# Second MLP products of the last half with tokens on partitions, in a two-layer encoder kernel

## The chip, the cores and the metric

The kernel runs on one core of one Trainium2 chip. Its time is device time in microseconds (us) of one execution; repeated executions of a kernel agree within some tenths of a per cent. Before the change the median of three runs is 1166.66 us (1165.98 to 1166.71).

## The reference

The input is one sequence of 512 tokens with 1024 channels, float32. Two layers follow each other; each has a mixer and an MLP, each wrapped in two RMS norms:

```python
x = x + rms_norm(m, g[1])                      # m: the layer's mixer on rms_norm(x, g[0])
h = rms_norm(x, g[2])
x = x + rms_norm(squared_relu_mlp(h, mlp_w1[i], mlp_w2[i]), g[3])

def squared_relu_mlp(h, w1, w2):               # 1024 -> 4096 -> 1024
    return jnp.square(jax.nn.relu(h @ w1)) @ w2

def conformer_conv(h, w_pw1, b_pw1, w_dw, b_dw, ln_g, ln_b, w_pw2, b_pw2):
    u = h @ w_pw1 + b_pw1                      # 1024 -> 2048
    a, g = jnp.split(u, 2, axis=-1)
    u = a * jax.nn.sigmoid(g)
    u = depthwise_conv(u, w_dw) + b_dw         # over tokens, centred, 31 wide
    u = jax.nn.silu(layer_norm(u, ln_g, ln_b))
    return u @ w_pw2 + b_pw2
```

Layer 0's mixer is a gated short convolution beside latent attention with 8 heads, with a shared input and a shared output projection. Layer 1's mixer is `conformer_conv`. The result is x after layer 1, float32.

## The kernel before

**Layout.** Channels lie on partitions and tokens along the free axis: x, the norm's output h, the MLP's hidden values and the sub-layer's output m are each 8 tiles of 128 channels by up to 512 tokens. A product therefore has a 128 x 128 block of a weight as the stationary operand and the tokens of one half as the moving one.

**Precision.** Every large product is made from three: a value is split into a part that the fast float32 mode of TensorE holds (`whi`, the high part of x) and a rest (`wlo`). `linear` (L252) and `mm` (L244) issue high x high, high x low and low x high, lines 248, 249 and 250, for each of eight blocks of input channels: 24 products make one output tile of 128 channels. This is called a step here.

**Weights.** `strip` (L212) loads 512 KB of weights on SP's queue (`raw`), copies the high part on ScalarE (L225) and subtracts the rest on GpSimd (L226). There are eight buffers for `whi` and eight for `wlo`. `take` (L552) asks for strips ahead of the step that uses them, as many as `AHEAD` says for the stage.

**Halves.** Work on the sequence is cut in two halves, A and B, so that one half's norms run beside the other half's products. Ahead of the depthwise convolution the halves are tokens 0 to 255 and 256 to 511. The convolution of A's last tokens would need 15 tokens of B, so behind it A2 is tokens 0 to 239 and B2 is 240 to 511 (`PAD` = 16, L118).

**Order.** The list M2 (L36) is the order of the middle part, and M3 (L37) of the last. An item is a run of steps (`up`: first MLP product of one of four groups of 1024 hidden channels, with relu, square and split; `down`: second product of that group, added to m; `pw1`, `pw2`: the convolution module's projections) or a chain of small work for one half (`join`: post-norm, add, next pre-norm; `norm`: the layer norm behind the convolution; `finish`: the last post-norm, add and store). While a chain is written out, `hold` and `pace` (L305 to L316) draw steps of the other half that come next in the list, so that TensorE has products beside it. The convolution is 31 multiply-adds per channel block on VectorE; `fill` (L278) credits each step with some microseconds (`FILL`) and puts in as many of the multiply-adds as the credit buys at the prices of `TAP_US`. What is left when `norm` begins is put in between further drawn steps, with `STEP_US - OP_US` = 1.96 us credited for each. The order on VectorE is the order written; on the other engines a planner may move an instruction ahead of one that it holds to be late.

**Accumulators.** Of the eight PSUM banks three are named S, two pj, one o and two mi. Products of `linear` go round S and pj, norms and transposes use o and mi.

**The end.** The last group of B2 ends with `down` (L535): add to m on VectorE, square on ScalarE, add to a sum, multiply by the post-norm's gain on ScalarE. `finish_step` (L952) then forms the column sums with products against ones (L370), the reciprocal root in small VectorE operations (`rstd`, L386 to L428), spreads it over partitions with products against the identity (L435), multiplies m by it and adds it to x, five of the eight tiles on VectorE and three on GpSimd, and stores each tile.

Of the kernel before, what the change touches and what calls it, by code (L numbers as in the profile page):

```python
# [35 lines left out]
M2 = [('up', 'A', 0, 0, 0, 8), ('join', 'B', 0, 1), ('down', 'A', 0, 0, 0, 8), ('up', 'A', 0, 1, 0, 8), ('down', 'A', 0, 1, 0, 8), ('up', 'A', 0, 2, 0, 8), ('down', 'A', 0, 2, 0, 8), ('up', 'A', 0, 3, 0, 8), ('down', 'A', 0, 3, 0, 8), ('join', 'A', 0, 3), ('up', 'B', 0, 0, 0, 8), ('down', 'B', 0, 0, 0, 4), ('pw1', 'A', 0, 8), ('down', 'B', 0, 0, 4, 8), ('up', 'B', 0, 1, 0, 8), ('down', 'B', 0, 1, 0, 8), ('up', 'B', 0, 2, 0, 2), ('norm', 'A'), ('up', 'B', 0, 2, 2, 8), ('down', 'B', 0, 2, 0, 8), ('pw2', 'A', 0, 8), ('join', 'A', 1, 1), ('up', 'B', 0, 3, 0, 8), ('down', 'B', 0, 3, 0, 8), ('join', 'B', 0, 3), ('up', 'A', 1, 0, 0, 8), ('down', 'A', 1, 0, 0, 4), ('pw1', 'B', 0, 8), ('down', 'A', 1, 0, 4, 8), ('up', 'A', 1, 1, 0, 8), ('down', 'A', 1, 1, 0, 8), ('up', 'A', 1, 2, 0, 6), ('norm', 'B'), ('up', 'A', 1, 2, 6, 8), ('down', 'A', 1, 2, 0, 8), ('up', 'A', 1, 3, 0, 4), ('pw2', 'B', 0, 8), ('join', 'B', 1, 1), ('up', 'A', 1, 3, 4, 8), ('down', 'A', 1, 3, 0, 8), ('up', 'B', 1, 0, 0, 8), ('down', 'B', 1, 0, 0, 6), ('finish', 'A'), ('down', 'B', 1, 0, 6, 8), ('up', 'B', 1, 1, 0, 8), ('down', 'B', 1, 1, 0, 8), ('up', 'B', 1, 2, 0, 8), ('down', 'B', 1, 2, 0, 8)]  # L36
M3 = [('up', 'B', 1, 3, 0, 8), ('down', 'B', 1, 3, 0, 8), ('finish', 'B')]  # L37
# [4 lines left out]
TAP_US = {T // 2 - PAD: (0.385, 0.51), T // 2 + PAD: (0.41, 0.54)}  # L42
# [9 lines left out]
IN_ORDER = ('M3',)  # L52
POOL_OUT = {'A': (), 'B': (0, 1, 2)}
AHEAD = {'m0': 7, 'm1': 2, 'm2': 4, 'm3': 5}
RAWS = {'m1': 4, 'm2': 4, 'm3': 1}
RAW0 = {'m1': 8, 'm2': 4, 'm3': 8}
# [34 lines left out]
class Seg:  # L91
# [28 lines left out]
STARTS = [0, 128, 256, 384, 112, 240, 368]  # L120
# [13 lines left out]
def trunk(ctx: ExitStack, tc: tile.TileContext, a, out: bass.AP):  # L134
# [32 lines left out]
    def accum():  # L167

        scope["turn"] += 1
        tags = [t for t in scope["acc"] if t != "pj" or not (convs or todo or scope.get("chain"))]  # L170
        return ps(tags[scope["turn"] % len(tags)])
# [4 lines left out]
    def scratch(w):  # L176
# [3 lines left out]
        tags = ["o", "pj", "mi", "pj"] if scope.get("chain") else ["o", "mi"]  # L180
# [5 lines left out]
    def ht(dt=F32):  # L186
        return new(ap, "h", 2 * NC, T + PAD, dt=dt)[:, :T]
# [4 lines left out]
    def hpair():  # L192
        return tuple(Win(new(ap, "h", 2 * NC, T + PAD, dt=F32R)) for _ in range(2))
# [6 lines left out]
    vec = cp.tile([P, NV], F32, name="vec")  # L200
    ident = kst[:, K_ID : K_ID + P]
# [70 lines left out]
    late, convs, todo, normed, credit, turn = [], [], [], [], [0.0], [0]  # L272
# [191 lines left out]
    def join(xs, ms, s, post, pre, hs, seg, h, mlp):  # L464
# [4 lines left out]
        hv = views(hs, seg)  # L469
# [51 lines left out]
    def up(w, hs, dst, seg):  # L521

        acc = linear(w, views(hs, seg), seg, whole=True)
# [631 lines left out]
```

## Time and profile before

| what | value |
|---|---|
| profiled execution, its own time | 1166.52 us |
| its span, first to last instruction | 1164.6 us |
| granted TensorE clock, mean | 0.996 |
| TensorE products (PE) | 1132.3 us busy, 8850 instructions |
| weight loads into TensorE (PEld) | 1093.1 us, 8850 |
| GpSimd (POOL) | 846.2 us, 409 |
| ScalarE (ACT) | 663.8 us, 1221 |
| VectorE (DVE) | 645.7 us, 1696 |
| read from HBM | 180.42 MB |

A line of the profile that names an operation reads: line of the kernel, engine, operation, tile written <- tiles read, then shapes and a count with x. Behind a bar stand the busy time in us, the mean duration of one in ns, and the time that the engine sat idle just ahead of these instructions, with what ended it. In a timeline the first two numbers are the start and the duration in us, and square brackets hold the idle time ahead and its releaser. In a table of windows the columns are the stretch, its length, the busy time of each engine asked for (with its instructions), the granted clock, the share of the DMA engines and GB/s. Products overlap each other: the duration of one is longer than the distance to the next.

### The profile page before, as it was taken

Reading aid. Unit: us, or ns where it says so; the run is one execution under the profiler, and the core shown is the slowest. Engines: PE = TensorE matmul, PEld = TensorE weight load, DVE = VectorE, ACT = ScalarE, POOL = GpSimd, SP = SyncE. Lnnn points to the kernel's source line nnn. Section 1 sums busy time; section 2 is a strip of 40 time slices with the busy share of each in tenths; the row PEclk is TensorE's granted clock in tenths of the full one; section 3 lists DMA queues with packets and bytes.
Section 4 is the critical chain, followed back from the end, with each engine's and each line's share of the span. In section 5 each row is a group of like instructions: output and inputs, shape, how many; then the busy total and the mean of one; then the engine's idle time right before and its main releaser. Section 6 shows DMA issues by size and latency. Waiting matters only on the chain.

```text
span 1164.6 us, 22863 instructions
## 1 busy us (share of the span) xinstructions
PE 1132.3 (97%) x8850; PEld 1093.1 (94%) x8850; DVE 645.7 (55%) x1696; ACT 663.8 (57%) x1221; POOL 846.2 (73%) x409
## 2 busy tenths in 40 slices
PE   7999989999999999999999999999999999999995
PEld 5788868999999999999999999999999999999995
DVE  5662699554522124499985265599985272322123
ACT  6531677466745457645566778546467685545352
POOL 5663563149988888598886978698887877887681
PEclk9999999999999999999999999999999999999998
DMA  6421332036656555366554555465655554653431
GB/s 209 156 85 30 101 106 73 1 116 231 205 179 198 182 180 187 126 219 195 178 188 161 182 181 191 151 212 192 198 182 181 173 174 161 213 179 123 150 131 39
DMA packets 55405, 183.99 MB, mean 158 GB/s; under 512 B 6401, under 2 KB 10881, under 8 KB 55297
## 3 DMA queue, kind: packets, MB, share of 16 engines
q1 hardware_dynamic: 54720, 181.86, 47.9%
q8 instruction: 69, 1.13, 0.4%
q10 hardware_dynamic: 576, 0.68, 0.2%
q14 instruction: 40, 0.32, 0.1%
HBM read 180.42 MB, written 2.10 MB: 157 GB/s over the span
## 4 chain that ended last, share of the span: by engine, by line
PE 92%; DVE 3%; ACT 3%; DMA 1%; issue 1%; POOL 0%; SPq 0%; POOLq 0%; ACTq 0%
PE S L248 23%; PE S L249 23%; PE S L250 22%; PE pj L248 7%; PE pj L249 7%; PE pj L250 7%; DVE pr L772 1%; PE mi L370 1%; PE mi L435 1%; ACT whi L225 1%; PE mi L775 1%; DVE s L766 1%; PE o L249 1%; PE o L250 0%; DVE pt L238 0%
## 5 line engine op out<-in xcount | busy, mean ns | idle before, releaser
L226 POOL TENSOR_TENSOR wlo<-raw,whi 128x1024 fp32r<-128x1024 f32 (+2 forms) x347 | 802.9, 2335 | 252.2 <-ACT whi L225 243.3
L225 ACT ACTIVATE whi<-raw 128x1024 fp32r<-128x1024 f32 (+2 forms) x347 | 355.7, 1031 | 378.0 <-PE S L249 176.6
L248 PE MATMUL S<-h,whi 128*128 128x256 f32 (+3 forms) x1216 | 346.8, 289 | 6.2 <-ACT h L232 3.4
L250 PE MATMUL S<-h,wlo 128*128 128x256 f32 (+3 forms) x1216 | 349.9, 289 | 0.0
L249 PE MATMUL S<-h,whi 128*128 128x256 f32 (+3 forms) x1216 | 349.8, 289 | 0.1
L248 PEld LDWEIGHTS S<-h,whi 128*128 128x128 f32 x1216 | 227.5, 189 | 12.2 <-ACT h L232 4.2
L249 PEld LDWEIGHTS S<-h,whi 128*128 128x128 f32 x1216 | 229.4, 189 | 4.3 <-DVE h L235 0.5
L250 PEld LDWEIGHTS S<-h,wlo 128*128 128x128 f32 x1216 | 229.5, 189 | 4.0 <-POOL wlo L226 0.3
L248 PE MATMUL S<-hid,whi 128*128 128x256 f32 (+2 forms) x824 | 230.3, 282 | 2.0 <-DVE acc L335 1.8
L249 PE MATMUL S<-hid,whi 128*128 128x256 f32 (+2 forms) x824 | 230.7, 281 | 0.0
L250 PE MATMUL S<-hid,wlo 128*128 128x256 f32 (+2 forms) x824 | 230.0, 280 | 0.0
L837 DVE SCALAR_TENSOR_TENSOR pj<-u,taps,pj 128x240 f32<-128x240 f32 (+1 forms) x464 | 192.4, 481 | 1.3
L248 PEld LDWEIGHTS S<-hid,whi 128*128 128x128 f32 x824 | 154.5, 189 | 2.8 <-DVE acc L335 2.2
L249 PEld LDWEIGHTS S<-hid,whi 128*128 128x128 f32 x824 | 155.4, 189 | 0.2 <-DVE hid L238 0.2
L250 PEld LDWEIGHTS S<-hid,wlo 128*128 128x128 f32 x824 | 155.4, 189 | 0.0
L248 PE MATMUL pj<-h,whi 128*128 128x272 f32 (+3 forms) x336 | 103.6, 308 | 6.9 <-ACT h L232 5.5
L249 PE MATMUL pj<-h,whi 128*128 128x272 f32 (+3 forms) x336 | 103.1, 307 | 0.0
L250 PE MATMUL pj<-h,wlo 128*128 128x272 f32 (+3 forms) x336 | 102.8, 306 | 0.0
L248 PEld LDWEIGHTS pj<-h,whi 128*128 128x128 f32 x336 | 63.7, 190 | 10.1 <-ACT h L232 5.8
L238 DVE TENSOR_TENSOR hid<-S,hid 128x256 fp32r<-128x256 f32 (+2 forms) x103 | 43.1, 419 | 51.2 <-ACT hid L232 50.9
L540 DVE TENSOR_TENSOR m<-S,m 128x256 f32<-128x256 f32 (+2 forms) x74 | 30.6, 416 | 65.3 <-PE S L250 65.3
L249 PEld LDWEIGHTS pj<-h,whi 128*128 128x128 f32 x336 | 63.6, 189 | 3.4 <-DVE h L235 0.9
(247 smaller groups left out, 1683.1 us busy)
## 6 DMA issues: line engine op xcount, KB each, us to landing
raw<-in_w SPq DMA_DIRECT2D x256, 512.0 KB, 3.4
raw<-in_pw SPq DMA_DIRECT2D x48, 512.0 KB, 3.4
raw<-in_win SPq DMA_DIRECT2D x16, 512.0 KB, 3.3
x<-in_xT SPq DMA_DIRECT2D x16, 256.0 KB, 4.2
raw<-in_wout SPq DMA_DIRECT2D x8, 512.0 KB, 3.3
raw<-in_wq SPq DMA_DIRECT2D x8, 192.0 KB, 2.4
out<-x SPq DMA_DIRECT2D x8, 120.0 KB, 2.6
out<-x SPq DMA_DIRECT2D x5, 136.0 KB, 1.7
```

What stands on the lines that cost most here:

```text
L225: nc.scalar.activation(h, r, AF.Copy)
L226: nc.gpsimd.tensor_tensor(out=lo[:, c0:c1], in0=r, in1=h.bitcast(F32), op=ALU.subtract)
L238: eng.tensor_tensor(out=lo, in0=src, in1=hi.bitcast(F32), op=ALU.subtract)
L248: nc.tensor.matmul(acc, sh, mh, start=i == 0, stop=False)
L249: nc.tensor.matmul(acc, sh, ml, start=False, stop=False)
L250: nc.tensor.matmul(acc, sl, mh, start=False, stop=i == n - 1)
L370: nc.tensor.matmul(s[:, b : b + 1], q[:, sl.start - self.seg.lo : sl.stop - self.seg.lo], one, start=i == 0, stop=i == len(self.parts) - 1,)
L435: nc.tensor.matmul(o[:, sl], r[:, b : b + 1].to_broadcast([bw, P]), ident[:bw, :bw], start=True, stop=True,)
L540: nc.vector.tensor_tensor(out=m[seg.sl], in0=acc, in1=m[seg.sl], op=ALU.add)
L766: nc.vector.reduce_max(out=mx, in_=S, axis=AX.X)
L772: eng.tensor_scalar(out=pr_, in0=pr_, scalar1=sm, scalar2=None, op0=ALU.mult)
L837: nc.vector.scalar_tensor_tensor(out=dst, in0=src, scalar=wk, in1=acc, op0=ALU.mult, op1=ALU.add)
```

## The change

**The last half's second products.** For B2 in layer 1 the `down` items become `turn` and `end`. The hidden tile's 128 x 128 block (128 hidden channels by 128 tokens) is now stationary, and 512 columns of a row strip of w2 are moving; the result has tokens on partitions and output channels along the free axis. Four banks are open through a group, one for each of two blocks of 128 tokens and two halves of the output channels (two S, two pj). A strip of w2 (128 hidden channels by 1024 outputs) serves 12 products. At a group's end the four banks are copied (ScalarE, first group) or added (VectorE) to tiles m of 128 x 512, which take the place of the convolution's u tiles.

**The residual.** A new item `residual` transposes x for B2 on TensorE, four times four blocks, and ScalarE copies the four banks into further u tiles.

**The end.** The last group goes by blocks of 128 tokens: all products of block 0 first, strip by strip, with all eight strips kept; then block 1, first its first 512 output channels, then its last 512 in two halves of 256. Each piece is added to m on VectorE, squared and summed along the free axis on ScalarE, and multiplied by the gain on GpSimd (a tile of the gain on all partitions is loaded once, on ScalarE's queue). The sum is then one number per partition, so the reciprocal root multiplies m directly in one operation that also adds the residual, and the rows are stored to a second output; the host puts the two outputs together.

**The halves.** Behind the convolution the halves are now 0 to 255 and 256 to 511, ahead of it 0 to 271 and 272 to 511. The shifted views of h are no longer needed. The stage M3 with its own buffers is gone: everything is in M2. `finish` now serves A alone and is done on VectorE.

```diff
-M2 = [...]
-M3 = [('up', 'B', 1, 3, 0, 8), ('down', 'B', 1, 3, 0, 8), ('finish', 'B')]
+M2 = [... ('up', 'B', 1, 0, 0, 8), ('turn', 'B', 1, 0, 0, 6), ('finish', 'A'), ('turn', 'B', 1, 0, 6, 8), ('up', 'B', 1, 1, 0, 8), ('residual', 'B'), ('turn', 'B', 1, 1, 0, 8), ('up', 'B', 1, 2, 0, 8), ('turn', 'B', 1, 2, 0, 8), ('up', 'B', 1, 3, 0, 8), ('end', 'B', 1, 3)]
...
-TAP_US = {T // 2 - PAD: (0.385, 0.51), T // 2 + PAD: (0.41, 0.54)}
+TAP_US = {T // 2: (0.395, 0.525)}
...
-AHEAD = {'m0': 7, 'm1': 2, 'm2': 4, 'm3': 5}
+AHEAD = {'m0': 7, 'm1': 2, 'm2': 4}
...
-HALVES = A, B = Seg(0, T // 2), Seg(T // 2, T)
-A2, B2 = Seg(0, T // 2 - PAD), Seg(T // 2 - PAD, T, PAD)
+HALVES = A, B = Seg(0, T // 2 + PAD), Seg(T // 2 + PAD, T)
+A2, B2 = Seg(0, T // 2), Seg(T // 2, T)
...
+    def banks_step(h, g):
+        if not turned:
+            for key in BLOCKS:
+                turned[key] = [None, tmp("u")[:, :T], tmp("u")[:, :T]]
+            turned["gain"] = gtok
+        for n, key in enumerate(BLOCKS):
+            turned[key][0] = ps(("S", "pj")[n % 2])
+    def turn_mm(acc, h, w, k, b, cols, n):
+        tok = slice(T // 2 + b * P, T // 2 + b * P + P)
+        x, c = hid[h][k], slice(cols.start + n, cols.stop + n)
+        return [
+            (acc[:, cols], x[0][tok], w[0][:, c], k == 0, False),
+            (acc[:, cols], x[0][tok], w[1][:, c], False, False),
+            (acc[:, cols], x[1][tok], w[0][:, c], False, k == NC - 1),
+        ]
+    def turn_step(tok, h, layer, g, k):
+        if k == 0:
+            banks_step(h, g)
+        w = take()
+        for b in range(2):
+            issue([turn_mm(turned[b, f][0], h, w, k, b, slice(0, T), f * T) for f in range(2)])
+        settle()
+        if k == NC - 1:
+            for key in BLOCKS:
+                acc, m, _ = turned[key]
+                if g == 0:
+                    nc.scalar.activation(m, acc, AF.Copy)
+                else:
+                    nc.vector.tensor_tensor(out=m, in0=acc, in1=m, op=ALU.add)
+    def residual_step(tok, h, b, f):
+        tp = misc()
+        lo = T // 2 + b * P
+        for i in range(NB):
+            nc.tensor.transpose(tp[:, i * P : (i + 1) * P], xs[f * NB + i].t[:, lo : lo + P], ident)
+        nc.scalar.activation(turned[b, f][2], tp, AF.Copy)
+    def end_step(tok, h, layer, g):
+        f12 = lack.pop(h)
+        banks_step(h, g)
+        ws = []
+        for k in range(NC):
+            ws.append(take())
+            issue([turn_mm(turned[0, f][0], h, ws[k], k, 0, slice(0, T), f * T) for f in range(2)])
+            settle()
+        parts = {b: [] for b in range(2)}
+        def piece(b, f, cols):
+            acc, m, _ = turned[b, f]
+            acc, m, g = acc[:, cols], m[:, cols], turned["gain"][:, f * T + cols.start : f * T + cols.stop]
+            nc.vector.tensor_tensor(out=m, in0=acc, in1=m, op=ALU.add)
+            sm = small(1)
+            nc.scalar.activation(acc, m, AF.Square, accum_out=sm)
+            nc.gpsimd.tensor_tensor(out=m, in0=m, in1=g, op=ALU.mult)
+            parts[b].append(sm)
+        def leave(b, r, n):
+            w = T // n
+            for f in range(2):
+                for i in range(n):
+                    m, x = (t[:, i * w : i * w + w] for t in turned[b, f][1:])
+                    nc.vector.scalar_tensor_tensor(
+                        out=x, in0=m, scalar=r, in1=x, op0=ALU.mult, op1=ALU.add
+                    )
+                    q = nc.scalar if i % 2 else nc.sync
+                    q.dma_start(out_b[b * P : (b + 1) * P, f * T + i * w : f * T + i * w + w], x)
+        def rest(f, cols):
+            for k in range(NC):
+                issue([turn_mm(turned[1, f][0], h, ws[k], k, 1, cols, f * T)])
+        for f in range(2):
+            piece(0, f, slice(0, T))
+        rest(0, slice(0, T))
+        r = root(0)
+        leave(0, r, 1)
+        piece(1, 0, slice(0, T))
+        for i in range(2):
+            cols = slice(i * T // 2, (i + 1) * T // 2)
+            rest(1, cols)
+            piece(1, 1, cols)
+        leave(1, root(1), 2)
...
+    nc.scalar.dma_start(gtok, a["gain"].to_broadcast([P, D]))
```

More of the change, by code (lines that the diff above doesn't have):

```diff
@@ L133, in trunk @@
 @with_exitstack
-def trunk(ctx: ExitStack, tc: tile.TileContext, a, out: bass.AP):
+def trunk(ctx: ExitStack, tc: tile.TileContext, a, out: bass.AP, out_b: bass.AP):
     nc = tc.nc
@@ L169, in accum @@
         scope["turn"] += 1
-        tags = [t for t in scope["acc"] if t != "pj" or not (convs or todo or scope.get("chain"))]
+        tags = [t for t in scope["acc"] if t != "pj" or turned or not (convs or todo or scope.get("chain"))]
         return ps(tags[scope["turn"] % len(tags)])
@@ L179, in scratch @@
         scope["scr"] += 1
-        tags = ["o", "pj", "mi", "pj"] if scope.get("chain") else ["o", "mi"]
+        tags = ["o", "pj", "mi", "pj"] if scope.get("chain") and not turned else ["o", "mi"]
         return ps(tags[scope["scr"] % len(tags)])[:, :w]
@@ L192, in hpair @@
     def hpair():
-        return tuple(Win(new(ap, "h", 2 * NC, T + PAD, dt=F32R)) for _ in range(2))
+        return tuple(Win(new(ap, "h", 2 * NC, dt=F32R)) for _ in range(2))
     def small(w=NB):
@@ L200, in trunk @@
     vec = cp.tile([P, NV], F32, name="vec")
+    gtok = cp.tile([P, D], F32, name="gtok")
     ident = kst[:, K_ID : K_ID + P]
@@ L521, in up @@
     def up(w, hs, dst, seg):
-        acc = linear(w, views(hs, seg), seg, whole=True)
+        acc = linear(w, hs, seg, whole=True)
         cols = slice(seg.lo, seg.lo + seg.n)
@@ L794, in trunk @@
         else:
-            attend(h, A if half == "A" else B)
+            attend(h, A2 if half == "A" else B2)
     ycat = ya + yb
@@ L930, in pw2_step @@
             sums[h] = Sum(NC, seg, whole=WHOLE[3])
-        acc = linear(take(), views(hs, seg), seg)
+        acc = linear(take(), hs, seg)
         nc.scalar.activation(ms[m][seg.sl], acc, AF.Identity, bias=col(V_BPW2 + m))
@@ L954, in finish_step, with add @@
         bc = rstds(sums[h], lack.pop(h))
[L955 to L971 removed]
+        def add(j, x, t):
+            nc.vector.tensor_tensor(out=x, in0=x, in1=t, op=ALU.add)
+            nc.sync.dma_start(out[j * P : (j + 1) * P, :], x)
+        for j in range(NC):
+            x, m = xs[j][seg.sl], ms[j][seg.sl]
+            t = scratch(seg.w)
+            nc.vector.tensor_tensor(out=t, in0=m, in1=bc, op=ALU.mult)
             settle()
@@ L975, in finish_step @@
         settle()
+    BLOCKS = [(b, f) for b in range(2) for f in range(2)]
+    def banks_step(h, g):
[13 more added lines that the diff above has]
+        ]
@@ new lines, in issue @@
+    def issue(lists):
+        for products in zip(*lists):
+            for acc, x, w, start, stop in products:
+                nc.tensor.matmul(acc, x, w, start=start, stop=stop)
+    def turn_step(tok, h, layer, g, k):
[12 more added lines that the diff above has]
+                    nc.vector.tensor_tensor(out=m, in0=acc, in1=m, op=ALU.add)
@@ L995, in run @@
                     add(down_step, h, *args, m)
+            elif what == "turn":
+                need(a["w2t"][args[1], k] for k in range(args[2], args[3]))
+                for k in range(args[2], args[3]):
+                    add(turn_step, h, *args[:2], k)
+            elif what == "residual":
+                for b, f in BLOCKS:
+                    add(residual_step, h, b, f)
+            elif what == "end":
+                need(a["w2t"][args[1], k] for k in range(NC))
+                add(end_step, h, *args)
             elif what == "wout":
@@ L1000, in run @@
                     add(shared_step, h, lambda: ycat, seg_of(h, 0), True, m)
-            elif what == "attend":
-                add(lambda tok, h, half: attend(h, A if half == "A" else B), *args)
             elif what == "pw1":
@@ L1044, in trunk @@
     run(M2)
-    ph.__exit__(None, None, None)
-    ph = phase("m3", raw=("raw2", RAWS["m3"], STRIP), **MLP)
-    run(M3, "M3" in IN_ORDER)
     ph.__exit__(None, None, None)
```

60 lines of the change are left out of this document (28 added, 32 removed).

## The prediction, made before the changed kernel ran

> **What bounds the kernel now.** First the page: busy times, then the chain that ended last.
>
> ```profile
> span 1164.6 us, 22863 instructions
> PE 1132.3 (97%) x8850; PEld 1093.1 (94%) x8850; DVE 645.7 (55%) x1696; ACT 663.8 (57%) x1221; POOL 846.2 (73%) x409
> ...
> PE 92%; DVE 3%; ACT 3%; DMA 1%; issue 1%; POOL 0%; SPq 0%; POOLq 0%; ACTq 0%
> ```
>
> PE is 92% of the chain: time is products times their pace, plus the places where PE stands, plus the tail behind the last product. The pace comes from three stretches with products of one width (busy time by windows: 256, 272 and 240 columns), and two rows of the first phase 18 products apart (512 columns).
>
> ```profile
> 340.00:400.00 60.00, 60.00 (x512) 1.00 0.60 194
> 960.00:1020.00 60.00, 60.00 (x483) 1.00 0.58 185
> 790.00:850.00 60.00, 60.00 (x535) 1.00 0.59 194
> ...
> 70.67 0.40 PE L248 MATMUL S<-h,whi 128*128 128x512 f32 x1
> ...
> 74.81 0.40 PE L248 MATMUL pj<-h,whi 128*128 128x512 f32 x1
> ```
>
> A count includes about two products under way at the window's start, so one product costs 60/510 = 0.1176 us at 256 columns, 60/481 = 0.1247 at 272, 60/533 = 0.1126 at 240; at 512 it is 4.14/18 = 0.230. A step (24 products) is 2.82, 2.99 and 2.70 us. A pair of unequal halves costs 5.69, an equal pair 5.64; 512 columns save 0.005 against two of 256.
>
> **The products.** Ahead of the convolution 88 step pairs (8 output projection, 64 MLP, 16 pw1) go from equal to unequal: 88 x 0.05 = +4.4 us. Behind it 40 pairs (8 pw2, 32 up) go the other way: -2.0. The 32 down steps of A grow from 240 to 256 columns: +3.8. The 32 down steps of B cost 32 x 2.99 = 95.7; they become 24 strips of 12 products at 512, 24 x 2.76 = 66.2, and the end: 72 at 512 and 48 at 256, 16.6 + 5.6 = 22.2. That is -7.3. Sum **-1.1**. No row has this pairing (a hidden tile stationary, weights moving), only the 512-wide rows above; at 0.226 it would be -2.5, at two 256-wide products' 0.235 it would be +0.7.
>
> In the old order a group's first down step reads all eight hidden tiles within 3 us, and PE waits for the last one:
>
> ```profile
> 1127.61 0.28 PE L250 MATMUL S<-hid,wlo 128*128 128x272 f32 x1
> 1127.89 1.05 ACT L225 ACTIVATE whi<-raw 128x1024 fp32r<-128x1024 f32 x1
> 1128.03 0.44 DVE L238 TENSOR_TENSOR hid<-S,hid 128x272 fp32r<-128x272 f32 x1 [0.46 <-ACT hid L232]
> 1128.05 0.52 PE L248 MATMUL S<-hid,whi 128*128 128x272 f32 x2 [0.15 <-ACT hid L232]
> ```
>
> 0.44 us between products instead of 0.125. The new order needs hidden tile 7 only after 7 x 2.76 us: **-0.3**.
>
> **Weights.** DMA, ACT and POOL work per strip stays (32 strips of 512 KB). The end takes its eight strips at 6 x 0.230 = 1.38 us each, faster than POOL splits them:
>
> ```profile
> 1062.63 1.06 ACT L225 ACTIVATE whi<-raw 128x1024 fp32r<-128x1024 f32 x1 [0.73 <-PE S L249]
> ...
> 1063.78 2.40 POOL L226 TENSOR_TENSOR wlo<-raw,whi 128x1024 fp32r<-128x1024 f32 x1 [0.59 <-ACT whi L225]
> ```
>
> But ACT waits here for PE to leave a buffer, so all eight buffers are full. At the end's start seven strips are there; the eighth follows after 0.1 + 1.06 + 2.40 = 3.6 us and is wanted at 7 x 1.38 = 9.7. Cost 0. Without that cover, with only the four asked for ahead, POOL would finish the eighth at 1.06 + 4 x 2.4 = 10.7: 1.0 late. The gain's 512 KB broadcast goes out on ACT's queue between the phases, where full buffers hide it; uncovered it is one strip's load:
>
> ```profile
> raw<-in_w SPq DMA_DIRECT2D x256, 512.0 KB, 3.4
> ```
>
> **The residual's transposes** are new: 16 on PE, four copies of 512 columns on ACT. The nearest are attention's:
>
> ```profile
> 214.59 0.87 PE mi L775 x8
> ...
> L232 ACT ACTIVATE pt<-mi 128x512 fp32r<-128x512 f32 x32 | 18.8, 595 | 2.5 <-PE mi L775 1.9
> ```
>
> 16 x 0.109 = 1.75 us of PE. There are two mi banks: set 3 waits for copy 1. The order is planned with other products ready, so I add only 0.35, **+2.1**; from 1.75 up to 4.0, if sets 3 and 4 each stand for a copy behind a whi (0.60 + 1.06, less 0.5).
>
> **Where the convolution shifts work.** A convolves 256 columns instead of 240, B 256 instead of 272. Taps, DVE's load in both convolutions, and the start of A's pw2:
>
> ```profile
> L837 DVE SCALAR_TENSOR_TENSOR pj<-u,taps,pj 128x272 f32<-128x272 f32 x232 | 100.4, 497 | 0.7
> L837 DVE SCALAR_TENSOR_TENSOR pj<-u,taps,pj 128x240 f32<-128x240 f32 x232 | 92.0, 464 | 0.6
> ...
> 500.00:610.00 110.00, 103.22 (x272) 1.00 0.61 195
> 757.00:872.00 115.00, 111.23 (x274) 1.00 0.60 196
> ...
> 630.41 0.61 PE L435 MATMUL mi<-kst,s 128*128 128x128 f32 x4
> ...
> 631.06 1.03 DVE L869 TENSOR_TENSOR m<-m,mi 128x240 f32<-128x240 f32 x3 [1.64 <-PE mi L435]
> ...
> 632.86 0.49 PE L248 MATMUL S<-h,whi 128*128 128x240 f32 x2 [1.85 <-ACT h L232]
> ```
>
> A tap is 0.397 us at 240, 0.433 at 272, so about 0.415 at 256: A's 248 add 4.5 us to DVE, which is 94% busy there (103.2 of 110), while B's filler steps shrink from 2.82 to 2.70. The planner credits 8 x 4.8 + 4 x 2.6 + 18 x 2.3 = 90.2 us ahead of A's norm and charges 8 x 32 turns at 0.385 = 98.6 now, at 0.395 = 101.1 after; with the dearer price while a channel is alone, and 1.96 us credited per drawn step, that draws 6 filler steps into the rest of the convolution now and 8 after, of 14; six instead of eight are left for its layer norm, and none once the second root is asked for. So PE, which already stands 1.85 us at pw2 A, loses 2 x 2.7 = 5.4 us of cover; but with nothing queued on PE the norm's small products answer sooner. Between 0 and +5.4; I take +2.3, somewhat below half. B's side gains: a step more of cover behind its norm, and 256 instead of 240 columns under B's join, where DVE is late for PE:
>
> ```profile
> 897.72 0.52 PE L248 MATMUL S<-h,whi 128*128 128x272 f32 x2 [0.34 <-ACT h L232]
> ...
> 944.08 0.38 PE L248 MATMUL S<-hid,whi 128*128 128x240 f32 x1 [1.27 <-DVE acc L335]
> 947.57 0.38 PE L248 MATMUL S<-hid,whi 128*128 128x240 f32 x1 [0.53 <-DVE acc L335]
> ```
>
> Of the 1.8 us in the last two rows I take 1.2 back (0 to 1.8) and 0.3 at the norm (0 to 0.34). The join of A ahead of pw1 draws 11 filler steps that are each 0.12 shorter: 0 to 1.3, taken 0.4, as PE runs through most of that join without a stand. Sum **+1.2**, from -2.1 to +6.7.
>
> **The end.** The tail now:
>
> ```profile
> 1149.94 0.29 PE L250 MATMUL pj<-hid,wlo 128*128 128x272 f32 x1
> 1150.26 0.44 DVE L540 TENSOR_TENSOR m<-pj,m 128x272 f32<-128x272 f32 x1 [2.22 <-PE pj L250]
> ...
> 1150.74 0.40 ACT L360 ACTIVATE pj<-m 128x272 f32<-128x272 f32 x1 [2.05 <-DVE m L540]
> ...
> 1152.59 0.17 DVE L393 TENSOR_TENSOR mi<-mi,fB 128x3 f32<-128x3 f32 x1 [0.98 <-PE mi L370]
> ...
> 1155.08 0.16 DVE L428 TENSOR_TENSOR s<-mi,fB 128x3 f32<-128x3 f32 x1
> ...
> 1159.61 2.19 POOL L963 TENSOR_TENSOR x<-x,m 128x272 f32<-128x272 f32 x3
> ```
>
> PE is through at 1149.94 + 0.125 = 1150.07, so the tail is 14.5 us: sums, column sums, root, spread, a copy, eight tiles of multiply and add, then 2.8 from POOL's last add (1161.80) to 1164.6. The new pieces' durations:
>
> ```profile
> L540 DVE TENSOR_TENSOR m<-S,m 128x256 f32<-128x256 f32 x36 | 15.0, 419 | 35.3 <-PE S L250 35.3
> L479 DVE SCALAR_TENSOR_TENSOR pj<-pj,vec,x 128x256 f32<-128x256 f32 x16 | 7.7, 484 | 0.0
> ...
> L360 ACT ACTIVATE S<-m 128x256 f32<-128x256 f32 x20 | 7.6, 382 | 0.4 <-DVE m L540 0.3
> ...
> L769 ACT ACTIVATION_READ_ACCUMULATOR pr<-S,s 128x1 f32 x32 | 6.3, 196 | 0.0
> ```
>
> New tail: hand-over 0.19, add 0.42, hand-over and square 0.44, accumulator 0.20, hand-over and sum of three 0.25, root 2.65 (1152.59 to 1155.24), hand-over 0.1, four fused multiply-adds at 0.40 and a last at 0.48, so 1.68, and 2.8 as before: 8.7. **-5.8**, give or take 0.5. Block 0's epilogue (adds, root, two wide multiply-adds, about 7 us) runs under block 1's 72 products (11 us); POOL's multiply by the gain under the root.
>
> The last quarter is made in two halves of one PSUM bank, with DVE's add and ACT's square (which writes back into that bank) between. If the bank is guarded as a whole, PE's 24 last products wait 0.19 + 0.42 + 0.44 + 0.1 = **+1.2**; if columns are told apart, 0. Nothing but DVE's last add is queued behind. In the rows above a reader of a bank starts only after PE's last product into it (L540 after L250), so I take the guard. By the Trainium skill (PSUM — Partial Sum Buffer, "PSUM bank collisions raise a hardware error") two engines on one bank collide even at disjoint columns, and semaphores must guard by bank; by that rule the sum has the 1.2, without it not; no run here shows it yet.
>
> **Sum:** -1.1 - 0.3 + 2.1 + 1.2 - 5.8 + 1.2 = -2.7 on the profiled 1166.5 us (span 1164.6 and 1.9 around it; the runs' median is 1166.66, 0.1 off): **1163.8**.
>
> **Rivals.** (1) The bank isn't waited for and A's norm loses nothing: 1163.8 - 1.2 - 2.3 = 1160.3. For: planning fills holes; against: 1.85 us are lost there already. (2) A's convolution falls behind: the whole 5.4, 1163.8 + 3.1 = 1166.9. For: 94% plus 4.5 us is nearly full; against: B runs at 111.2 of 115 and PE stays fed. (3) Slower: the swapped products can't hold 0.230, because the hidden tile is now the one loaded into PE and 512 weight columns stream from the buffers that ACT and POOL fill. At 0.250, 360 x 0.020 = +7.2: 1171.0. It decides from 0.245 on (360 x 0.015 = 5.4 takes the forecast past 1169.0). For: the 512-wide rows come from a quiet phase; against: 256-wide rows keep their pace under load. (4) The swap buys nothing: 0.235 per 512 columns (+1.8) and transposes at 4.0 (+1.9): 1167.5.
>
> **Chances.** Forecast 0.50 (own range 1161 to 1166), rivals 0.19, 0.12, 0.09, 0.10. 0.2% is 2.3 us, about what this measurement can tell from no change, so "faster" is below 1164.3 and "slower" above 1169.0. Faster: 0.34 of the forecast and rival 1, 0.53. Same: 0.16 of the forecast, 0.09 of rival 2, 0.07 of rival 4, 0.32. Slower: rival 3 and 0.03 each of 2 and 4, 0.15. Range **1159.5 to 1168.0**: it leaves out rival 3, the top of 2 and 4, and the bottom of 1.
>
> **What would show it.** Tail of 8.7 us from the last product; 0.230 between 512-wide products at the end; 1.2 us of PE idle ahead of its last 24 products, released by ACT; PE's wait at pw2 A near 4 us instead of 1.85, and smaller waits in B's join; no POOL wait in the end. A tail above 11, or a pace above 0.24, makes the forecast wrong.

## The result and the profile after

The changed kernel takes 1172.88 us (median of four runs, 1171.0 to 1174.89) beside 1166.68 us of the kernel before in the same comparison: 1.0053 times as long, interval 1.0035 to 1.0072. It is **6 us slower**; the forecast was 1163.8 us and its range ended at 1168.0. The profiled execution spans 1171.7 us, 7.1 more than before.

Page of the changed kernel: busy times and the chain that ended last.

```profile
span 1171.7 us, 22121 instructions
PE 1134.6 (97%) x8492; PEld 1081.3 (92%) x8492; DVE 649.2 (55%) x1693; ACT 661.5 (56%) x1211; POOL 846.0 (72%) x408
...
PE 85%; DVE 6%; ACT 3%; DMA 3%; POOL 1%; issue 1%; SPq 0%; DVEq 0%; ACTq 0%; POOLq 0%
```

PE is still the bound, but the chain leaves it for 15% of the span instead of 8%. To see where the 7.1 us arise, take the start of the same relu in both traces (there are 128, eight per group and half, numbered from 0). After minus before, with the work between in words:

| at | after minus before, us | what lies ahead of it |
|---|---|---|
| first relu | +4.1 | attention's last step, output projection of A, join |
| relu 48 | +13.6 | first MLP of A (272 columns instead of 256: comes back under B) |
| relu 64 | +17.1 | layer norm of A behind the convolution |
| relu 96 | +20.5 | layer 1, A with 256 columns instead of 240 |
| last relu | +10.9 | layer 1, B with 256 columns instead of 272, swapped products |
| end of span | +7.1 | last products and tail |

The wide swing is the new split itself, work moved between A and B. What does not come back sits in four places, and one place gives back.

**Ahead of the first MLP.** Timeline of PE in the changed kernel, with the idle time ahead in brackets, and one window (stretch, length, PE busy with its instructions, clock, DMA share, GB/s). The fence after it has the same window of the kernel before, and one that is used below.

```profile
225.18 0.38 PE L246 MATMUL o<-pt,h 128*128 128x256 f32 x1 [0.69 <-ACT pt L230]
225.90 0.39 PE L247 MATMUL o<-pt,h 128*128 128x256 f32 x1 [0.34 <-DVE pt L236]
227.93 0.52 PE L246 MATMUL S<-ycat,whi 128*128 128x272 f32 x2 [0.47 <-ACT ycat L230]
259.96 0.38 PE L246 MATMUL S<-ycat,whi 128*128 128x240 f32 x1 [0.64 <-DVE acc L333]
...
220.00:230.00 10.00, 8.50 (x66) 1.00 0.01 2
```

```profile
220.00:230.00 10.00, 9.97 (x85) 1.00 0.01 2
634.00:644.00 10.00, 10.00 (x91) 1.00 0.18 57
```

Before, A's output projection needs the tokens 0 to 255, that is A's attention alone, and its products fill PE while the last attention step (head 7, B) goes through its softmax. Now A is 0 to 271: sixteen of its tokens belong to the attention half 256 to 511, so the projection's last channel block waits for that very step. PE stands 0.69 + 0.34 + 0.47 = 1.5 us around that step and 0.64 us in B's projection, 2.1 us in all. Another 1.4 us are A's projection itself, 192 products at 0.125 instead of 0.118, which B's narrower one mostly returns. The 0.6 us that are left of the 4.1 are not accounted for.

**A's layer norm, and the clock behind it.** The PE rows in which it stands, and two windows (the sixth number is the granted clock):

```profile
642.15 0.58 PE L368 MATMUL mi<-kst,acc 128*128 128x1 f32 x4 [0.53 <-DVE acc L333]
645.04 1.22 PE L433 MATMUL mi<-kst,s 128*128 128x128 f32 x4 [2.32 <-DVE s L419]
648.17 1.01 PE L246 MATMUL S<-h,whi 128*128 128x256 f32 x3 [1.91 <-ACT h L230]
...
644.20:654.20 10.00, 7.25 (x32) 0.50 0.27 93
654.40:664.40 10.00, 10.00 (x86) 1.00 0.22 70
```

Before, PE stands there once, 1.85 us at 632.86. Now it stands 0.53 + 2.32 + 1.91 = 4.76, so +2.9. Behind it, from 644.1 to 654.3, the clock is granted at half: 28 of the 32 products in that window are full ones, and they come every 0.213 us instead of 0.120, 28 x 0.093 = **2.6 us** more. Before, the same place runs at full clock (634 to 644 us, above).

**The pace of 256-wide products.** Two copies of a hidden tile's high part (the instruction behind each relu), five steps apart (5 x 24 products, all with h moving), in layer 1:

```profile
984.71 0.39 ACT L230 ACTIVATE hid<-S 128x256 fp32r<-128x256 f32 x1 [0.50 <-DVE S L525]
...
999.11 0.38 ACT L230 ACTIVATE hid<-S 128x256 fp32r<-128x256 f32 x1 [0.50 <-DVE S L525]
```

14.40 us for 120 products is 0.1200 each, where 256 columns took 0.1176 before. With the hidden tiles moving they stay at 0.118 to 0.119, as before.

**The end.** Two rows from a block of swapped products, and then the last products and the tail:

```profile
1065.64 0.39 PE L990 MATMUL S<-whi,hid 128*128 128x512 f32 x1
...
1066.80 0.39 PE L990 MATMUL pj<-wlo,hid 128*128 128x512 f32 x1
```

```profile
1159.44 0.38 PE L990 MATMUL pj<-whi,hid 128*128 128x256 f32 x1 [1.06 <-ACT pj L1031]
...
1162.30 0.28 PE L990 MATMUL pj<-whi,hid 128*128 128x256 f32 x1
1162.68 0.42 DVE L1029 TENSOR_TENSOR u<-pj,u 128x256 f32<-128x256 f32 x1 [3.83 <-PE pj L990]
1163.14 0.39 ACT L1031 ACTIVATE pj<-u 128x256 f32<-128x256 f32 x1 [3.75 <-DVE u L1029]
1163.46 0.19 ACT L1031 ACTIVATION_READ_ACCUMULATOR pj<-u 128x1 f32 x1
1163.68 0.79 DVE L1039 SCALAR_TENSOR_TENSOR mi<-s,s,s 128x1 f32<-128x1 f32 x1 [0.58 <-ACT pj L1031]
...
1164.50 0.17 DVE L391 TENSOR_TENSOR mi<-mi,fB 128x1 f32<-128x1 f32 x1
...
1167.22 1.67 DVE L1051 SCALAR_TENSOR_TENSOR u<-u,s,u 128x256 f32<-128x256 f32 x4
```

Five products in 1.16 us: 0.232. PE stands 1.06 us ahead of the last 24 products, released by ScalarE, which with the products' restart is 1.2 in distance. From the last product's end (1162.42) to 1171.7 the tail is 9.3 us; before it was 14.5.

Together: 2.1 + 2.9 + 2.6, 1920 products (64 first steps of layer 1 and 16 of pw2, 24 each) at 0.0018 to 0.0024 more = 3.5 to 4.6, 1.2 of bank wait, less 5.2 of tail: 7.1 to 8.2 us, for 7.1 found; the parts are not known to much better than 1 us. The forecast's other terms (-1.1, -0.3, +2.1, -1.2, -0.3, +0.4) add to -0.4.

### The profile page after: what moved, and what is told of

It is laid out like the page before. It is cut to its first block, busy times and chain, and to the rows that moved or that the text cites. A ratio compares the mean times of both kernels' runs of the same rounds, so it can differ in the third digit from the quotient of the medians.

```text
span 1171.7 us, 22121 instructions
## 1 busy us (share of the span) xinstructions
PE 1134.6 (97%) x8492; PEld 1081.3 (92%) x8492; DVE 649.2 (55%) x1693; ACT 661.5 (56%) x1211; POOL 846.0 (72%) x408
## 4 chain that ended last, share of the span: by engine, by line
PE 85%; DVE 6%; ACT 3%; DMA 3%; POOL 1%; issue 1%; SPq 0%; DVEq 0%; ACTq 0%; POOLq 0%
PE S L246 20%; PE S L247 19%; PE S L248 19%; PE pj L246 5%; PE pj L247 5%; PE pj L248 5%; PE pj L990 4%; PE S L990 4%; DMA raw<-in_win 2%; POOL wlo L224 1%; ACT whi L223 1%; DVE pr L767 1%; DMA raw<-in_w 1%; PE mi L433 1%; PE mi L770 1%
## 5 line engine op out<-in xcount | busy, mean ns | idle before, releaser
L832 DVE SCALAR_TENSOR_TENSOR pj<-u,taps,pj 128x256 f32<-128x256 f32 x464 | 192.6, 484 | 1.3
L246 PE MATMUL S<-hid,whi 128*128 128x256 f32 (+2 forms) x664 | 185.3, 281 | 1.4 <-DVE acc L333 1.2
L248 PE MATMUL S<-hid,wlo 128*128 128x256 f32 (+2 forms) x664 | 186.5, 282 | 0.0
L247 PE MATMUL S<-hid,whi 128*128 128x256 f32 (+2 forms) x664 | 186.3, 281 | 0.0
L246 PEld LDWEIGHTS S<-hid,whi 128*128 128x128 f32 x664 | 124.8, 189 | 2.5 <-DVE acc L333 1.8
L248 PEld LDWEIGHTS S<-hid,wlo 128*128 128x128 f32 x664 | 125.3, 189 | 0.0
L247 PEld LDWEIGHTS S<-hid,whi 128*128 128x128 f32 x664 | 125.3, 189 | 0.0
L246 PE MATMUL pj<-h,whi 128*128 128x256 f32 (+3 forms) x344 | 105.5, 307 | 9.5 <-ACT h L230 7.6
L248 PE MATMUL pj<-h,wlo 128*128 128x256 f32 (+3 forms) x344 | 105.3, 306 | 0.3 <-POOL wlo L224 0.3
L247 PE MATMUL pj<-h,whi 128*128 128x256 f32 (+3 forms) x344 | 105.3, 306 | 0.0
L246 PEld LDWEIGHTS pj<-h,whi 128*128 128x128 f32 x344 | 65.5, 191 | 12.4 <-ACT h L230 7.6
L247 PEld LDWEIGHTS pj<-h,whi 128*128 128x128 f32 x344 | 65.5, 190 | 3.4 <-DVE h L233 1.1
L248 PEld LDWEIGHTS pj<-h,wlo 128*128 128x128 f32 x344 | 65.6, 191 | 3.1 <-POOL wlo L224 0.7
```

The source lines that it names most:

```text
L246: nc.tensor.matmul(acc, sh, mh, start=i == 0, stop=False)
L247: nc.tensor.matmul(acc, sh, ml, start=False, stop=False)
L248: nc.tensor.matmul(acc, sl, mh, start=False, stop=i == n - 1)
L832: nc.vector.scalar_tensor_tensor(out=dst, in0=src, scalar=wk, in1=acc, op0=ALU.mult, op1=ALU.add)
```

## The experiments

Differences in us are the difference of the ratios to the kernel before, times 1166.7. The changed kernel itself has four runs and an interval of +-2.1 us, so a single difference from it is no better than that. The kernel before was timed again beside each group of runs and took 1167.6 to 1168.7 us there, so the ratios are to be compared and not the absolute times. The first theory was the last section's: the halves lose, the end gains. Its rival: the swapped products or the end are what is slow.

**1. The halves alone**, with the old products, the old end and the old tile widths.

```diff
 (kernel before)
-TAP_US = {T // 2 - PAD: (0.385, 0.51), T // 2 + PAD: (0.41, 0.54)}
+TAP_US = {T // 2: (0.395, 0.525)}
-HALVES = A, B = Seg(0, T // 2), Seg(T // 2, T)
-A2, B2 = Seg(0, T // 2 - PAD), Seg(T // 2 - PAD, T, PAD)
+HALVES = A, B = Seg(0, T // 2 + PAD), Seg(T // 2 + PAD, T)
+A2, B2 = Seg(0, T // 2), Seg(T // 2, T)
...
-            attend(h, A if half == "A" else B)
+            attend(h, A2 if half == "A" else B2)
```

> The kernel before with the new halves alone (272/240 ahead of the convolution, 256/256 behind, its prices and block starts), everything else old: down steps, M3, finish, h tiles with 16 spare columns. Theory (the halves cost the time): output projection of A waits for the last attention head (about +3.5 us by the first relu), the stand at pw2 A grows from 2 to about 6 us, and the clock is granted at half for 10 us behind it (+5): about 1178. Rival (the new products and the new end cost it): no change, 1167 to 1168, clock 0.996.

Measured 1174.01 us, ratio 1.0050 (1.0030 to 1.0069): **+5.8 us**, as much as the whole change. Its trace has the same stands (2.31 and 1.91 us at A's norm) with 6.83 us of half clock, 8.51 us of PE in the window from 220 to 230 us, and the first relu 4.2 us later. That is half of the loss expected: 10 us at half clock had been taken as 5 us more, and the trace above shows 2.6, because PE stands for part of them. The loss needs neither the swapped products nor the new end; with the pace of 0.232 above, rival 3 of the prediction falls.

**2 and 3. Cover for A's norm**: steps of B put ahead of the second pointwise product of A, one and four of them.

```diff
 (changed kernel; run 3 shown, run 2 has 1 in place of 4)
-('down', 'B', 0, 2, 0, 8), ('pw2', 'A', 0, 8), ('join', 'A', 1, 1), ('up', 'B', 0, 3, 0, 8)
+('down', 'B', 0, 2, 0, 8), ('up', 'B', 0, 3, 0, 4), ('pw2', 'A', 0, 8), ('join', 'A', 1, 1), ('up', 'B', 0, 3, 4, 8)
```

> The changed kernel with pw2 A one up step of B later, so that one step more covers A's layer norm. Theory (a stand beyond some length costs a second time, by the clock): the stands around the norm fall from 5.9 to about 3.2 us, and if that is short enough for the clock the time falls by 2.7 + 5 to about 1165; if not, by 2.7 to about 1170. Rival (clock drop unrelated to the stand): 1170 with a half clock somewhere.

> The changed kernel with pw2 A four up steps of B later, as B's own pw2 has it in the list. Theory: the stand at the norm goes to under 1 us and no half clock follows: 5 + 5 us less, about 1163, clock 0.996 or more. Rival (the clock drop has another cause): about 1168, clock 0.993.

Measured 1.0025 (1.0014 to 1.0037) with one step and 1.0004 (0.9995 to 1.0013) with four: -3.3 and **-5.7 us** against the changed kernel. One step did not do what was expected: PE still stands 2.32 and 1.90 us there, with 6.83 us of half clock. The run with four, PE's one stand and the window behind it:

```profile
656.26 0.39 PE L246 MATMUL S<-h,whi 128*128 128x256 f32 x1 [1.27 <-ACT h L230]
...
658.60:661.80 3.20, 3.20 (x17) 0.50 0.53 169
```

The stand is 1.27 us instead of 4.76, and only 3.41 us of half clock follow instead of 10.24. Between the first relu and relu 64 this trace is 3.8 us shorter than the changed kernel's. In the place where I had taken +2.3, stand and clock together are worth 4 to 6 us, and the 1.27 us that are left still cost a stretch of half clock, where none was expected.

**4. The idle time filled** with eleven products that nothing reads (six beside the root, five behind its spread), to part the idle time from the clock.

```diff
 (changed kernel, in layer_norm)
-        rb = rstds(s2)
+        r = rstd(s2.done(), D, busy=busy if seg is A2 else None)
+        rb = spread(r, seg)
+        if seg is A2:
+            busy(r, 5)
```

> The changed kernel with eleven products that nobody reads put into the two stands around A's layer norm (six behind the column sums, five behind the spread, float32, 256 columns); the norm's chain stays as long as it was. Theory: PE isn't idle, so no half clock follows; the time falls by about 5 to 1168 though nothing of the chain is shorter. Rival (the stand itself is the whole cost, the half clock comes anyway): 1173 or a little above.

Measured 1178.4 us, 1.0082 (1.0066 to 1.0098), and **inconclusive**: the planner put the norm's other products elsewhere, PE stood 3.22 us up to 644.83 ahead of the fillers, and 6.83 us of half clock came all the same. The fillers themselves then took 5.4 us at half clock ahead of the spread and 2.3 us behind it. It only shows that unread products are not free.

**5. The width of the h tiles.** The kernel before keeps h in tiles of 528 columns, because its second half's views are shifted by 16; the change makes them 512. This puts the 528 back and changes nothing else.

```diff
 (changed kernel)
-        return new(ap, "h", 2 * NC, dt=dt)
+        return new(ap, "h", 2 * NC, T + PAD, dt=dt)[:, :T]
-        return tuple(Win(new(ap, "h", 2 * NC, dt=F32R)) for _ in range(2))
+        return tuple(Win(new(ap, "h", 2 * NC, T + PAD, dt=F32R)) for _ in range(2))
```

> The changed kernel with its h tiles 528 columns wide in memory, as before, instead of 512. The theory that the narrower tile slows the 256-wide products with h moving (apart by 0.120 us in the changed kernel, 0.118 before) expects 0.118 again and some 1920 products x 0.0018 = 3.5 us less, 1169.4 +-1.5; the rival, that the difference of pace is of the program's layout elsewhere or of the records, expects no change (1172.9).

Measured 1170.28 us, 1.0018 (1.0009 to 1.0028): **-4.1 us**. The same two copies:

```profile
984.66 0.39 ACT L230 ACTIVATE hid<-S 128x256 fp32r<-128x256 f32 x1 [0.50 <-DVE S L525]
...
998.84 0.39 ACT L230 ACTIVATE hid<-S 128x256 fp32r<-128x256 f32 x1 [0.50 <-DVE S L525]
```

14.18 us for 120 products, 0.1182 instead of 0.1200. The theory holds: the width of the h tiles in memory sets the pace of these products. It does not act on them alone. In the first phase the 432 products of 512 columns with h moving are 0.227 us apart in the changed kernel (18 of them in 4.09 us from 70.97) and 0.230 in this run and before, so there the narrow tile is the better one, by 1.4 us; at 240 and 272 columns the differences are below 0.001 us and nearly cancel. Priced by pace, the 528 columns are thus worth 3.5 us less 1.4; the measured 4.1 has about +-2.4. The width also moves where each tile, and what lies behind the tiles, begins, and no run tells these two apart or says why a width is better.

This kernel and run 1 have the same halves and the same tiles and differ in the products and the end alone: 1.0018 against 1.0050 is **-3.7 us for the swapped products and the new end** (+-2.5).

**6. The last quarter in one piece**, so that nothing waits for its bank.

```diff
 (changed kernel, end_step)
-        for i in range(2):
-            cols = slice(i * T // 2, (i + 1) * T // 2)
-            rest(1, cols)
-            piece(1, 1, cols)
+        rest(1, slice(0, T))
+        piece(1, 1, slice(0, T))
```

> The changed kernel with the last quarter's products of block 3 not cut in two parts of 256 columns: they come as one run of 512-wide products, so nothing waits for the bank half way (1.22 us of PE idle ahead of the last 24 products in the changed kernel). The theory that the wait is plain loss, but that the last addition and output then cover 512 columns instead of 256, expects 1171.7 to 1173; the rival, that the split earns more at the end than it costs, expects 1173.5 or more.

Measured 1171.26 us, 1.0032 (1.0020 to 1.0044): -2.4 us against the changed kernel, though the intervals touch. The trace is clearer. From the last relu to the last product it takes 20.95 us instead of 22.55, and the tail is no longer:

```profile
1159.94 0.40 PE L990 MATMUL pj<-whi,hid 128*128 128x512 f32 x1
1160.38 0.69 DVE L1029 TENSOR_TENSOR u<-pj,u 128x512 f32<-128x512 f32 x1 [3.76 <-PE pj L990]
1161.10 0.60 ACT L1031 ACTIVATE pj<-u 128x512 f32<-128x512 f32 x1 [3.72 <-DVE u L1029]
...
1164.77 1.67 DVE L1051 SCALAR_TENSOR_TENSOR u<-u,s,u 128x256 f32<-128x256 f32 x4
```

Add and square grow by 0.27 and 0.21 us, but three partial sums become two, whose addition takes under 0.2 us, where the addition of three took 0.79. The split of the bank is plain loss, 1.6 us in the trace.

**7. The last attention steps in another order**, 6 B, 6 A, 7 B, 7 A.

> The changed kernel with the last four attention steps in the order 6 B, 6 A, 7 B, 7 A instead of 6 A, 6 B, 7 A, 7 B. The theory that the loss of 4 us ahead of the first MLP is the output projection of A (tokens 0 to 271) waiting for B's last head expects that B's projection or the A part come earlier and the first relu 2 to 4 us sooner, 1169 to 1171; the rival, that both halves of the last head are needed anyway, expects no change (1172 to 1174).

Measured 1173.15 us, 1.0046 (1.0033 to 1.0059): no change. The window from 220 to 230 us has 8.52 us of PE, the changed kernel's 8.50. A's projection needs both halves of the last head, whichever is last, as the rival had it.

**8. Cover, wide tiles and whole quarter together** (runs 3, 5 and 6 in one kernel).

> The changed kernel with four products of B ahead of the second pointwise product of A (measured before at -4.0), h tiles 528 wide, and the last quarter whole. If the three causes add, 1172.9 - 4.0 - 3.5 - 0.5 = about 1164.9, below the kernel before by 1.8; if the pace is not the tile's width, about 1168.4.

Measured 1164.31 us, **0.9971 (0.9960 to 0.9982) of the kernel before, -3.4 us**. Single gains of 5.7, 4.1 and 2.4 would make 12.2 against the changed kernel; found are 9.6, and the three share that kernel's +-2.1. In its trace PE stands once at A's norm, and from there no half clock follows up to the end of the products:

```profile
657.86 0.38 PE L246 MATMUL S<-h,whi 128*128 128x256 f32 x1 [1.26 <-ACT h L230]
...
660.00:670.00 10.00, 10.00 (x87) 1.00 0.32 107
```

**9. A stand made in the kernel before**, by putting A's norm two steps later in the order: does the half clock follow there too?

```diff
 (kernel before)
-('up', 'B', 0, 2, 0, 2), ('norm', 'A'), ('up', 'B', 0, 2, 2, 8)
+('up', 'B', 0, 2, 0, 4), ('norm', 'A'), ('up', 'B', 0, 2, 4, 8)
```

> The kernel before with nothing but A's layer norm put two first products of B (2.84 us of TensorE each) later in the written order, so that its chain has 5.7 us less cover. The theory that such a stand costs its own length and, on top, a stretch of half clock behind it expects the wait ahead of A's second pointwise product near 7.5 us (1.85 before), a stretch of half clock of 6.8 to 10.2 us behind it, and 1166.7 + 5.7 + 3.4 to 5.1 = 1175.8 to 1177.5. The rival, that the half clock of the changed kernel is of something else in it, expects no stretch and 1172.4.

**A miss.** 1170.23 us, 1.0025 (1.0014 to 1.0036), but not by the expected path: A's stand shrank from 1.85 to 0.95 us, and no half clock came in the middle. In the trace 2.8 us are lost ahead of the first relu, where the order is unchanged (at most 1.7 by a stretch of half clock at 68.6, the rest is not accounted for), and 2.4 us turn up 240 us later, around B's norm, where PE stands in four places:

```profile
883.02 0.38 PE L248 MATMUL S<-hid,whi 128*128 128x240 f32 x1 [0.49 <-DVE m L540]
886.74 0.35 PE L248 MATMUL S<-h,whi 128*128 128x240 f32 x1 [0.76 <-DVE m L540]
901.16 0.39 PE L248 MATMUL S<-h,whi 128*128 128x272 f32 x1 [0.96 <-ACT h L232]
902.47 0.39 PE L248 MATMUL S<-h,whi 128*128 128x272 f32 x1 [0.31 <-ACT h L232]
```

Moving a chain in the order moves VectorE's whole later queue with it; it was no clean way to make a stand.

**10. The old end with the cover**: run 1 with four steps ahead of the second pointwise product of A.

> The kernel before with the new halves and the old end (which stood at 1.0050 of the kernel before), and four products of B ahead of the second pointwise product of A. Its h tiles are 528 wide. If cover and end are independent it stands 4 us below the halves alone, 1174.0 - 4.0 - 1168.4 + 1166.7 = about 1168.3; the changed kernel with cover, padded tiles and a whole last quarter stood at 1163.3, so the new end with a whole last quarter would be worth 5 us. The rival, that the gain of that kernel came from the cover together with the halves and not from the end, expects 1163 to 1165.

Measured 1170.98 us, 1.0025 (1.0014 to 1.0035). With the new end, its last quarter whole, the same halves, tiles and cover stood at 0.9971: the swapped products and the new end are worth 0.0054, **6.3 us** (+-1.8). In this kernel, too, one stand of 1.23 us at A's norm brings a stretch of half clock, which its partner, run 8, does not have, so up to 1.7 us of the 6.3 can be that. The rival, that the gain came from the cover alone, falls.

**11. Eight steps of cover instead of four** (on kernel 8).

> The changed kernel with padded tiles, a whole last quarter and eight instead of four products of B ahead of the second pointwise product of A. With four, TensorE still stood 1.42 us there. If that is lack of cover it goes and the time is 1163.3 - 1.4 = about 1162; if moving the second pointwise product makes the join behind it late, the wait comes back there and the time stays at 1163 to 1165.

Measured 1167.86 us, 1.0000 (0.9991 to 1.0008), 3.4 us worse than with four. The wait comes back at the join behind it, with 3.41 us of half clock from 724.5 on:

```profile
724.90 0.58 PE L246 MATMUL S<-h,whi 128*128 128x256 f32 x1 [2.20 <-DVE hid L236]
```

**12. Kernel 8 with the order of heads of run 7.**

> The changed kernel with padded tiles, a whole last quarter, four products of cover and the last four attention steps as 6 B, 6 A, 7 B, 7 A. Alone the order of the heads made 0.8 us, within the intervals of no change; the stand of 0.80 us behind the projection of A was gone in that run. If it adds, about 1162.5; if it is nothing, 1163.3.

Measured 1164.74 us, 0.9972 (0.9962 to 0.9982): the same as kernel 8.

**13. A stand in the kernel before, this time by taking cover away**: two steps of B from ahead of the second pointwise product of A to behind it.

```diff
 (kernel before)
-('down', 'B', 0, 2, 0, 8), ('pw2', 'A', 0, 8), ('join', 'A', 1, 1)
+('down', 'B', 0, 2, 0, 6), ('pw2', 'A', 0, 8), ('join', 'A', 1, 1), ('down', 'B', 0, 2, 6, 8)
```

> The kernel before with nothing but the second pointwise product of A put two products of B earlier in the written order (ahead of the last two of 'down B 0 2' instead of behind them), so that A's layer norm has less cover, as in the changed kernel. The theory that the stand at A's norm costs its own length, and a stretch of half clock in multiples of 3.41 us right behind it wherever it is long enough, expects a wait of 4 to 7 us in place of 1.85, 3.4 to 6.8 us of half clock behind it, and 1166.7 + 2.2 to 5.4 + 1.0 to 2.7 = 1170 to 1175, all without anything else of the change. The rival, that the half clock needs something else of the change, expects the stand and no stretch: 1169 to 1172, with full clock from 100 us to 1150 us.

Measured 1171.86 us, 1.0027 (1.0018 to 1.0036): **+3.2 us**. The trace shows the changed kernel's picture in the kernel before:

```profile
627.94 1.22 PE L435 MATMUL mi<-kst,s 128*128 128x128 f32 x4 [2.31 <-DVE s L421]
631.00 0.99 PE L248 MATMUL S<-h,whi 128*128 128x240 f32 x3 [1.85 <-ACT h L232]
...
627.80:634.40 6.60, 4.62 (x20) 0.50 0.35 122
```

PE stands 2.31 us more, and 6.83 us of half clock come with it. The stand needs nothing of the change, and neither does the clock.

**14. The order of heads of run 7 in the kernel before**: there it makes A's output projection wait for the last attention step, as it does in the changed kernel.

```diff
 (kernel before)
-(6, 'A'), (6, 'B'), (7, 'A'), (7, 'B')]
+(6, 'B'), (6, 'A'), (7, 'B'), (7, 'A')]
```

> The kernel before with the last four attention steps as 6 B, 6 A, 7 B, 7 A, so that A's output projection has to wait for the last attention step, as it does in the changed kernel, where it covers 16 tokens of B's half too. The theory that this dependence opens the stands around the last step (2.1 us between 225 and 228 us in the changed kernel, none before) expects stands of 1.5 to 3 us there, the first relu 1.5 to 3 us later, and 1168.2 to 1169.7. The rival, that the stands come from the widths of the halves and not from the dependence, expects 1166.7 and no stand above 0.5 us there.

Measured 1170.33 us, 1.0018 (1.0009 to 1.0027): **+2.1 us**, first relu 2.4 us later. Three of the changed kernel's four stands are there to the digit:

```profile
225.74 0.39 PE L248 MATMUL o<-pt,h 128*128 128x256 f32 x1 [0.69 <-ACT pt L232]
226.46 0.39 PE L249 MATMUL o<-pt,h 128*128 128x256 f32 x1 [0.34 <-DVE pt L238]
228.49 0.51 PE L248 MATMUL S<-ycat,whi 128*128 128x256 f32 x2 [0.47 <-ACT ycat L232]
...
220.00:230.00 10.00, 8.51 (x68) 1.00 0.01 2
```

The dependence opens these three, 1.5 us, and not the widths. The fourth, 0.64 us at B's projection, is missing here and in run 7, so it has another cause.

## Why the prediction was wrong

Three steps failed, all in what the new halves do, and each has its run.

1. **"Ahead of the convolution 88 step pairs ... go from equal to unequal"**: I priced the products of the moved boundary and not what their operands wait for. That A's tokens 256 to 271 come from the other attention half was in the diff, and the rows of 220 to 230 us before would have shown that A's projection is the cover of the last attention step. Missing term, **+2.1 us** (run 14, 1.0 to 3.2; in the changed kernel's trace 1.5 of the 2.1 us of stands are of this dependence).

2. **"Between 0 and +5.4; I take +2.3"** for A's norm. The place and the direction were right and the stand was +2.9. But it was priced as idle time alone. The half clock that came with it cost another 2.6 us in the profiled execution, and covering the place gave back 5.7 (run 3, +-2.4). A rule bears on this that I had not weighed: the Trainium skill (TensorE: Matmul & The Clock Gate, "What's actually happening") has the clock gated to half after idle windows of about 3.4 us that run free of the kernel. The stretches here are 3.41, 6.83 and 10.24 us long, multiples of that window, so the traces agree. They disagree on what it takes: the page asks for at least one idle window, and no stand was that long in runs 3, 11 and 13 (1.27, 2.20, 2.31 and 1.85 us).

3. **"One product costs ... 0.1176 us at 256 columns"** was carried over to tiles that the diff made narrower. The removed `T + PAD` stood in the diff, and I read it as memory saved. Mis-sized by 0.0018 to 0.0024 us on 1920 products, 3.5 to 4.6 us; run 5, which puts the width back, measures **4.1 us** (+-2.4). That the same tiles quicken the products of 512 columns by 1.4 us is neither in this term nor in the forecast.

The sum -2.7 + 2.1 + (2.9 + 2.6 - 2.3) + 4.1 is +6.7; measured +6.2. That they lie so close is in part luck: each of the measured terms is known to 1 to 2.4 us.

What held:

- The **tail**: 9.3 us for 8.7. Root to first multiply-add 2.72 (1164.50 to 1167.22) for 2.65 + 0.1, multiply-adds 1.67 for 1.68, and 2.8 behind them as before. The miss is the addition of three partial sums, 0.79 alone for an estimated 0.25 with its hand-over.
- The **pace** of the swapped products: 0.232 for 0.230, with no idle time on weights; rival 3 (0.250) and the weight side of rival 4 are out.
- The **bank wait**: 1.2 for 1.2, released by ScalarE. By the page of the Trainium skill that the prediction cites, the guard is by bank even at disjoint columns; the trace agrees, with 1.06 us of stand.
- The **transposes** stood for nothing: the range went to 4.0, and its lower end was right, 16 products 0.109 us apart, with no idle time ahead of them (last number of the group's row).

```profile
L1012 PE MATMUL mi<-kst,x 128*128 128x128 f32 x16 | 2.1, 272 | 0.0
```

- **B's join** gained less than taken. Its two waits in the changed kernel are

```profile
964.27 0.38 PE L246 MATMUL S<-hid,whi 128*128 128x256 f32 x1 [0.68 <-DVE acc L333]
967.93 0.39 PE L246 MATMUL S<-hid,whi 128*128 128x256 f32 x1 [0.56 <-DVE acc L333]
```

1.24 us instead of 1.80, so -0.6 for the forecast's -1.2.

For the swapped products and the end alone the forecast's terms, against run 1's shorter tail of 13.9 us, make -4.0: 32 steps at 256 columns (90.2 us) become 88.4, -0.3, +2.1, 13.9 to 8.7, +1.2. Measured -3.7 (+-2.5). The end was predicted; the halves that it needs were not.

What stays open: why the tiles' width in memory changes the pace, and whether it is the width or where the tiles begin; where exactly the clock's limit lies (the last section has what the traces show); and whether the 2.1 us at the last attention step can be had back: A's convolution needs those sixteen tokens, and another split of the attention was not tried.

## What to carry to other kernels

When a boundary is moved, list for each tile on the new side who makes it, and look in the trace for what the work that now waits had been covering. A stand on TensorE of more than a microsecond is to be priced with the half clock that can come with it, some 1.5 to 2.7 us here, and a few steps of cover win most of both back, while too many move the wait on. A tile's width in memory is part of a product's price: a diff that drops a pad is an edit to time by itself.

## What the runs showed of the hardware

- The half clock comes in stretches of 3.41 us and its multiples, which around A's norm begin between 1.0 us ahead of a stand's end and 2.3 us behind it, and products of 256 columns then come every 0.213 us instead of 0.120. The length of a stand does not settle it. Single stands of 1.27 and 1.23 us brought a stretch (runs 3 and 10), single stands of 1.26 and 1.25 us none (runs 8 and 12). The 1.85 us stand of the kernel before brought none in its own profile and one stretch in run 14, whose row there is the same:

```profile
635.77 0.49 PE L248 MATMUL S<-h,whi 128*128 128x240 f32 x2 [1.85 <-ACT h L232]
...
637.50:640.70 3.20, 3.20 (x17) 0.50 0.48 164
```

- What fits all of these is where the stand falls. Within a profile the changes of the clock lie whole multiples of 3.41 us apart, so the time can be cut into such windows. Runs 3 and 8, the window that holds most of the stand:

```profile
655.11:658.53 3.42, 2.12 (x12) 1.00 0.48 153
...
654.46:657.88 3.42, 2.16 (x20) 1.00 0.36 134
```

  The number behind the x is that of the products in the window: 12 in run 3's, and the next window is at half clock; 20 in run 8's, and the next is at full. Around A's norm and the join behind it, half clock followed on 12 to 15 products in runs 3, 10, 11, 13 and 14, and did not follow on 18 to 24 in the kernel before and in runs 8 and 12; a window without a stand holds about 30. In run 3 the stand and the slow products right behind it lie in one window; in run 8 the window ends with the stand, and in the kernel before the stand lies across two. No run moved a stand within the windows to test this.
- In some profiles, of several kernels, a single stretch of 3.41 us falls at 42 to 69 or near 155 us, ahead of the first MLP; it costs at most half its length, 1.7 us, and is part of the spread between executions.
- Products of 256 columns are 0.1200 us apart where their moving tile is 512 columns wide in memory, and 0.1182 where it is 528; products of 512 columns are 0.227 us apart with the first and 0.230 with the second.
- Splitting the last bank's columns to start its addition earlier cost 1.6 us in the trace, and the tail behind it was as long as without the split (9.4 and 9.3 us from the last product's start).
